# A hybrid decoder layer: the turn of x through six PSUM tiles, dt as one operand, and the SSD diagonal with features on partitions

## The chip, the cores and the metric

The kernel runs on one core of a Trainium2 chip. The core has five engines that run side by side and meet at semaphores: TensorE (PE, with its weight loads as PEld), VectorE (DVE), ScalarE (ACT), GpSimd (POOL) and SyncE (SP), which issues the DMAs here. [...] The metric is the device time of one execution in microseconds, as a median of several runs; the profile is of one further execution.

## The reference, cut to what matters

One layer over 16 learned meta tokens and 1024 tokens, width 1024, all in float32:

```python
xn = rms_norm(h, mix_pre_g)
proj = xn @ w_in                    # z, xBC, dt, q, k, v
# SSD (Mamba-2): 16 heads of 64, 2 groups, state 128, chunks of 128
xbc = silu(causal_dwconv(xbc, conv_w, conv_b))       # xs, B, C
dt = softplus(dt_raw + dt_bias); A = -exp(a_log)
Xdt = xs * dt; Acs = cumsum(dt * A, within a chunk)
Ldec = where(causal, exp(Acs[l] - Acs[s]), 0)
y_diag = einsum('bclgn,bcsgn,bgjcls,bcsgjp->bclgjp', C, B, Ldec, Xdt)
states = einsum(B, exp(Acs[-1] - Acs), Xdt)          # then a scan over the chunks: prev
y_off = einsum(C, prev, exp(Acs))
y_ssd = rms_norm((y_diag + y_off + xs * d_skip) * silu(z), ssd_norm_g)
y_sb = rms_norm(stick_breaking_attention(q, k, v), sb_norm_g)
h = h + rms_norm(concat(y_ssd, y_sb) @ w_out, mix_post_g)
h = h + rms_norm((gelu(dwconv3(xn2 @ W_g)) * (xn2 @ W_u)) @ w_down, ffn_post_g)
```

## The kernel before, in words

Activations and weights of the projections are split into a high part that PE takes in one pass (float32r) and a low rest, so that each product of two operands becomes three matmuls: high x high, low x high, high x low. Plain float32 matmuls stand in the profile as two records each; a transpose on PE is one record.

**Head.** The 1040 positions are nine tiles (16 meta tokens, then eight tiles of 128). For each (lines 204 to 222) ACT squares the tile and sums, DVE and POOL make the scaling factor (`rstd_of`), DVE writes `xn`, PE turns it in two halves of four 128x128 transposes into a PSUM tile of the tag "tp" (`xtp`, line 219), ACT writes the high part `xh` from there (line 221) and DVE the low rest `xl` (line 222). The tag "tp" has two tiles. In this first stage PSUM holds eight banks in four tags of two: "mm" (projections), "sd" (SSD outputs), "z" (masks and decays) and "tp" (turns).

**Projections.** `load_w` brings a block of 128 columns of weights and splits it (ACT high part, POOL low rest). `project_steps` walks three column chunks of 348, 346 and 346 positions (`CH`), 24 matmuls each, and calls `evac`. The first block is dt, only 16 columns wide; then come B and C of group 0, chunk by chunk in turn with dt. Convolutions over the positions run on DVE (`xbc_steps`, lines 313 and 316), silu on ACT.

**dt.** `dtT` (16 x 1040) is turned to tokens with nine transposes (`tpd`, line 390). Then a chain of some twenty small DVE instructions computes dt = softplus, dt x A (`adt`, tile `s2`, line 419) and its split. `decays()` multiplies `adt` with three triangular or full matrices (`pz_ea`, `pz_de`, `pz_cd`, lines 431 and 432) and takes exponentials on ACT. `fill` is a flow of projections of x blocks (`X`), of which two steps run ahead of `decays()`. `bc[0][1][0]()` turns B to tokens (`to_tokens`: `tt_B`, lines 324 and 329, three PSUM tiles of tag "tp", each copied by DVE at line 325 or 330).

**SSD scans.** Two groups of eight heads, nine chunks each (a meta chunk of 16 rows, eight of 128). `scan_steps` runs `chunk_weights(c + 1)`, `chunk_outputs(c)`, `chunk_store(c)` in turn, with steps of projections between. `chunk_weights` makes the decay mask (`sgh` on ACT, `sgl` on POOL, `sg` on PE, exp on ACT into `em`), multiplies it by the masked C.B products (`cb`, `cbm`) on DVE, and makes `xdt` (DVE) and `yo` = xs x d_skip (POOL); `em`, `xdt` and `yo` have two buffers each. `chunk_outputs` makes the state (`xw` on DVE, `st` on PE into a tile of tag "sd", `pv` on POOL and DVE), the diagonal (`yd`, line 507: eight matmuls with `em` as the stationary operand, 128 x 128, and 64 moving columns of `xdt`, into a tile of tag "sd"), adds it to `yo` on DVE (line 508), and the part from the state before (`yf`, line 511, also tag "sd"; `yt` and an addition on DVE). `chunk_store` turns `yo` to features (four transposes, `yt`, line 525), multiplies by silu(z) from `zk`, stores and sums squares.

**Order.** In this part of the kernel a scheduler sets each engine's order from the dependences and its own estimates; each engine then runs its queue strictly in order. From the attention on, PE's order is written by hand.

**Behind it** come eight head pairs of attention (a masked scan on DVE), the output projection, the norms, the up projections, the gated convolution and the down projections.

Of the kernel before, what the change touches and what calls it, by code (L numbers as in the profile page):

```python
# [8 lines left out]
F32 = mybir.dt.float32  # L9
# [7 lines left out]
P = 128  # L17
# [22 lines left out]
WB = 3  # L40
# [11 lines left out]
def tile_layer(ctx: ExitStack, tc: tile.TileContext, x, meta, rows, parts,  # L52
# [148 lines left out]
    with tc.tile_pool(name="pre", bufs=3, side="right") as pre:  # L201
        gpre = row_bcast(pre, 0, D, "gpre")
        for i in range(NT + 1):
            nr = NM if i == 0 else P
            c0 = 0 if i == 0 else NM + (i - 1) * P
            xt = pre.tile([P, D], F32, tag="xt", name=f"xt{i}", bufs=9)
            nc.sync.dma_start(out=xt[:nr], in_=meta if i == 0 else x[(i - 1) * P:i * P, :])
            junk = pre.tile([P, D], F32, tag="junk", name=f"junk{i}", bufs=2)
            ss = pre.tile([P, 1], F32, tag="ss", name=f"ss{i}")
            nc.scalar.activation(junk[:nr], xt[:nr], AF.Square, accum_out=ss[:nr])  # L210
            r = rstd_of(pre, ss[:nr], 1, nr, f"pre{i}")
            xn = pre.tile([P, D], F32, tag="xn", name=f"xn{i}", bufs=2)
            nc.vector.scalar_tensor_tensor(xn[:nr], xt[:nr], r[:nr], gpre[:nr],
                                           op0=ALU.mult, op1=ALU.mult)
            for hf in range(2):
                tp = psum_tp(f"xtp{i}_{hf}")
                for b in range(4):
                    k = 4 * hf + b
                    nc.tensor.transpose(tp[:, b, :nr], xn[:nr, k * P:(k + 1) * P], ident[:nr, :nr])
                dst = (slice(None), slice(4 * hf, 4 * hf + 4), slice(c0, c0 + nr))  # L220
                nc.scalar.activation(xh[dst], tp[:, :, :nr], AF.Copy)
                nc.vector.tensor_tensor(xl[dst], tp[:, :, :nr], xh[dst].bitcast(F32), op=ALU.subtract)
# [81 lines left out]
    with tc.tile_pool(name="ssd", bufs=1, side="right") as sp:  # L304
# [65 lines left out]
        expa = sp.tile([P, 16], F32, name="expa", tag="expa")  # L370
        nc.scalar.activation(expa, alog, AF.Exp)

        dtT = rp.tile([16, L + 3], F32, name="dtT", tag="rt", bufs=1)

        def dt_evac(acc, c0, n):
            nc.vector.tensor_copy(dtT[:, c0:c0 + n], acc[:16, :n])

        head = [project_steps(load_w(w_dt, 16, "dt"), 16, xh, xl, CH, dt_evac, "dt")]
        bc = bc_flow(0)
        head += [steps for steps, _ in bc]  # L380
        for _ in CH:
# [5 lines left out]
        for i in range(NT + 1):  # L387
            nr = NM if i == 0 else P
            c0 = 0 if i == 0 else NM + (i - 1) * P
            nc.tensor.transpose(tpd[:nr, i * 16:(i + 1) * 16], dtT[:, c0:c0 + nr], ident[:16, :16])  # L390
        NA = (NT + 1) * 16

        def t3(name, pool=sp):
# [40 lines left out]
                nc.scalar.activation(dst[:, 1:, :], pz[:, 16:NA].rearrange("p (a b) -> p a b", b=16), AF.Exp)  # L434

        fill = flow([x_flow(0, 0), x_flow(0, 1)], 2)
        run(fill, 2)
        decays()
        tmp.close()
        run(fill, 2)  # L440
        bc[0][1][0]()
        run(fill)

        def chunk_weights(g, c):
# [37 lines left out]
        def chunk_outputs(g, c, em, xdt, yo, prev):  # L482
# [8 lines left out]
            if c < NT:  # L491
# [8 lines left out]
                else:  # L500
# [1 line left out]
                                            prev.rearrange("p (h d) -> p h d", d=64),  # L502
                                            cdec[:, c, hs].unsqueeze(2).to_broadcast([P, 8, 64]), op=ALU.mult)
                    nc.vector.tensor_tensor(nprev, st, nprev, op=ALU.add)
            yg = psum_sd(f"yd{nm}").rearrange("p (h d) -> p h d", d=64)
            for h in range(8):
                mm(yg[:nr, h, :], em[:nr, h, :nr], xdt[:nr, h, :], start=True, stop=True)
            nc.vector.tensor_tensor(yo[:nr], yg[:nr], yo[:nr], op=ALU.add)
            if c > 0:
                yf = psum_sd(f"yf{nm}")  # L510
                mm(yf[:nr], ct[:, c0:c0 + nr], prev, start=True, stop=True)
# [3 lines left out]
                nc.vector.tensor_tensor(yo[:nr], yo[:nr], yt[:nr], op=ALU.add)  # L515
            return yo, zk, nprev

        def chunk_store(g, c, yo, zk):
            nr = NM if c == 0 else P
            c0 = 0 if c == 0 else NM + (c - 1) * P  # L520
            nm = f"{g}_{c}"
            tp = psum_tp(f"yt{nm}")
            yo2 = yo.rearrange("p h d -> p (h d)")
            for b in range(4):
                nc.tensor.transpose(tp[:, b, :nr], yo2[:nr, b * P:(b + 1) * P], ident[:nr, :nr])
            nc.vector.tensor_tensor(zk[:, :, :nr], tp[:, :, :nr], zk[:, :, :nr], op=ALU.mult)
            y0 = M0 if c == 0 else 0
            nc.sync.dma_start(out=yd[c][:, 4 * g:4 * g + 4, :], in_=zk[:, :, y0:nr])
            sqk = sp.tile([P, 4, P], F32, tag="sqk", name=f"sqk{nm}")
            nc.scalar.activation(sqk[:, :, :nr], zk[:, :, :nr], AF.Square)  # L530
            for b in range(0, 4, 2):
                nc.gpsimd.tensor_tensor(sqk[:, b, :nr], sqk[:, b, :nr], sqk[:, b + 1, :nr], op=ALU.add)
            dst = sq[:, c0:c0 + nr]
            if g == 0:
                nc.gpsimd.tensor_tensor(dst, sqk[:, 0, :nr], sqk[:, 2, :nr], op=ALU.add)
            else:
                nc.gpsimd.tensor_tensor(sqk[:, 0, :nr], sqk[:, 0, :nr], sqk[:, 2, :nr], op=ALU.add)
                nc.gpsimd.tensor_tensor(dst, dst, sqk[:, 0, :nr], op=ALU.add)

        def scan_steps(g):  # L540
# [3 lines left out]
            for c in range(NT + 1):  # L544
                nxt = chunk_weights(g, c + 1) if c < NT else None
                yield
                yo, zk, prev = chunk_outputs(g, c, *cur, prev)
                yield
                chunk_store(g, c, yo, zk)
                cur = nxt  # L550

        run(flow([x_flow(0, b) for b in range(2, 4)] + [(z_steps(0, b), []) for b in range(4)], 2))
# [1079 lines left out]
```

## Time and profile before

| | us |
|---|---|
| median of three runs | 1834.47 |
| lowest and highest | 1833.14 and 1835.4 |
| profiled execution, its own time | 1832.72 |
| its span, first to last instruction | 1831.0 |

The rows of the profile are read as follows. A row by stage gives the stretch in us from the span's start, its length, then for PE, PEld, DVE, ACT and POOL the busy time and in brackets the instructions, then the granted clock of TensorE as a share, the mean busy share of the DMA engines and GB/s. A row of waits gives the engine, tile and line that waited, then who ended it: the total, how often, the longest. A row in order of time gives the start, the duration, the engine, the line, the operation, the output <- the inputs, the forms and how many were merged; in brackets stands the idle time ahead of it and what ended it. For a matmul the pair before the form is contraction rows x stationary columns, and the form is rows x moving columns. Matmuls overlap, so two starts are compared rather than durations.

### The profile page before, as it was taken

The page shows a single profiled execution, that of the slowest core. Times are in us where ns is not written, and L with a number is a line of the kernel's source. Part 1 is how long each engine was busy: PE and PEld are TensorE (multiplying, and loading weights), DVE is VectorE, ACT ScalarE, POOL GpSimd, SP SyncE. Part 2 cuts the span into 40 slices and gives each one's busy share as a digit, 9 for nine tenths or more (in the row PEclk, how much of TensorE's full clock was granted, in tenths as well). Part 3 has the DMA queues.
Part 4 walks back from the last instruction along what each step waited for, and adds up shares of the span by engine and source line. Part 5 has one row for each costly group of instructions (what it writes and reads, how often), then busy time and mean ns, then how long its engine had stood idle before and what let it go on. Part 6 is the DMA issues. An engine that isn't in the chain of part 4 may idle for free.

```text
span 1831.0 us, 27362 instructions
## 1 busy us (share of the span) xinstructions
PE 1758.9 (96%) x10957; PEld 1508.3 (82%) x10957; DVE 1060.3 (58%) x1142; ACT 829.0 (45%) x1371; POOL 858.5 (47%) x613
## 2 busy tenths in 40 slices
PE   6899999999999999999799989899999999999997
PEld 5899889889888888888478767788889998888886
DVE  5551783574534544544722256766666666667988
ACT  5333454443655655655654243443333333344444
POOL 3213563485644644643764132276777776600001
PEclk9999999999999999999899999999999999999999
DMA  4123242231011110110232455233233333196344
GB/s 155 47 70 119 75 125 96 71 103 54 24 36 36 32 39 28 32 36 11 82 106 70 139 175 181 81 104 92 87 103 111 104 103 99 52 316 230 95 120 160
DMA packets 91443, 173.96 MB, mean 95 GB/s; under 512 B 11722, under 2 KB 36714, under 8 KB 91316
## 3 DMA queue, kind: packets, MB, share of 16 engines
q1 hardware_dynamic: 91316, 172.21, 29.9%
q8 instruction: 86, 1.41, 0.3%
q14 instruction: 41, 0.34, 0.1%
HBM read 122.39 MB, written 49.79 MB: 94 GB/s over the span
## 4 chain that ended last, share of the span: by engine, by line
PE 47%; DVE 3%; ACT 2%; POOL 1%; issue 1%; DMA 1%; POOLq 0%; SPq 0%; ACTq 0%; DVEq 0%
PE dn L1445 11%; PE fX L1054 9%; PE mo L759 6%; PE fY L1054 6%; PE fA L1054 6%; PE tw L617 1%; PE av L631 1%; PE z L596 1%; PE pj_v L163 1%; PE pj_q L163 1%; PE halo L708 1%; PE pj_k L163 1%; DVE oxn L912 1%; DVE mb L903 1%; POOL yl L749 0%
## 5 line engine op out<-in xcount | busy, mean ns | idle before, releaser
L601 DVE TENSOR_TENSOR_SCAN kp<-kp,hold 128x272 f32<-128x272 f32 (+7 forms) x128 | 206.7, 1657 | 202.3 <-ACT kp L597 99.6
L603 POOL TENSOR_TENSOR bt<-bt,kp 128x256 f32<-128x256 f32 (+7 forms) x128 | 213.8, 1688 | 195.9 <-DVE kp L601 143.3
L997 POOL TENSOR_TENSOR wl<-wr,wh 128x1024 fp32r<-128x1024 f32 x44 | 110.7, 2524 | 40.7 <-ACT wh L996 40.7
L1445 PE MATMUL dn<-dl,dh 128*128 128x512 f32 x308 | 120.1, 390 | 0.1
L1445 PE MATMUL dn<-dh 128*128 128x512 f32 x308 | 120.1, 390 | 0.0
L1445 PE MATMUL dn<-dh,dl 128*128 128x512 f32 x308 | 120.0, 390 | 0.0
L1491 POOL TENSOR_TENSOR fms<-fms,nhalf 128x1 f32<-128x1 f32 x8 | 8.5, 1060 | 225.8 <-DMA ar<-fda 186.0
L597 ACT ACTIVATE kp<-z 128x288 f32<-128x288 f32 (+6 forms) x112 | 82.7, 738 | 60.4 <-PE z L596 37.3
L1374 ACT ACTIVATE dh<-ar 128x512 fp32r<-128x512 f32 x77 | 48.7, 632 | 111.2 <-PE dn L1445 88.9
L996 ACT ACTIVATE wh<-wr 128x1024 fp32r<-128x1024 f32 x44 | 46.6, 1060 | 114.9 <-PE fX L1054 68.3
L596 PE MATMUL z<-k,q 64*128 64x144 f32 (+6 forms) x448 | 88.0, 494 | 8.3 <-ACT bt L598 3.9
L1126 DVE SCALAR_TENSOR_TENSOR ga<-gr,pp,ga 128x1024 f32<-128x1024 f32 x44 | 71.4, 1622 | 34.7 <-ACT ga L1119 34.0
L619 ACT ACTIVATE th<-tw 128x1024 f32<-128x1024 f32 (+2 forms) x96 | 74.4, 811 | 33.2 <-PE tw L617 31.1
L598 ACT ACTIVATE bt<-z 128x288 f32<-128x288 f32 (+6 forms) x112 | 83.0, 741 | 0.0
L617 PE MATMUL tw<-ident,bt 128*128 128x128 f32 x576 | 78.3, 282 | 4.4 <-POOL bt L603 2.9
L631 PE MATMUL av<-th,v 128*64 128x128 f32 x1152 | 78.1, 281 | 0.0
L631 PEld LDWEIGHTS av<-th,v 128*64 128x64 f32 x1152 | 62.6, 138 | 18.1 <-issue 17.3
L1375 DVE TENSOR_TENSOR dl<-ar,dh 128x512 fp32r<-128x512 f32 x77 | 53.2, 691 | 41.9 <-ACT dh L1374 41.8
L617 PEld LDWEIGHTS tw<-ident,bt 128*128 128x128 f32 x576 | 62.9, 143 | 15.9 <-issue 10.6
L596 PEld LDWEIGHTS z<-k,q 64*128 64x128 f32 x448 | 37.8, 191 | 39.0 <-issue 15.8
L1445 PEld LDWEIGHTS dn<-dh 128*128 128x128 f32 x308 | 57.8, 188 | 12.3 <-ACT dh L1374 0.3
L1445 PEld LDWEIGHTS dn<-dl,dh 128*128 128x128 f32 x308 | 57.9, 188 | 12.2 <-DVE dl L1375 0.4
(542 smaller groups left out, 5797.1 us busy)
## 6 DMA issues: line engine op xcount, KB each, us to landing
wr<-in_w_up SPq DMA_DIRECT2D x44, 512.0 KB
fds<-ga SPq DMA_DIRECT2D x44, 256.0 KB
b<-in_w_down SPq DMA_DIRECT2D x44, 256.0 KB
ar<-fds SPq DMA_DIRECT2D x44, 256.0 KB
fda<-ga SPq DMA_DIRECT2D x33, 256.0 KB
ar<-fda SPq DMA_DIRECT2D x33, 256.0 KB
yk<-yd SPq DMA_DIRECT2D x16, 512.0 KB
zd<-zt SPq DMA_DIRECT2D x8, 520.0 KB
```

Of the source, the lines that this page charges most:

```text
L596: mm(z[:, j, :w], q[h, t0:t0 + P], k[h, a:a + w], start=True, stop=True)
L597: nc.scalar.activation(kp[:, :, a:a + w], z[:, :, :w], AF.Sigmoid, scale=-QSCALE)
L598: nc.scalar.activation(bt[:, :, a:a + w], z[:, :, :w], AF.Sigmoid, scale=QSCALE)
L601: nc.vector.tensor_tensor_scan(kp[:, j][:, ::-1], kp[:, j][:, ::-1], hold[:, L - n:L][:, ::-1], 0.0, op0=ALU.mult, op1=ALU.max)
L603: nc.gpsimd.tensor_tensor(bt[:, j, 0:m], bt[:, j, 0:m], kp[:, j, 1:m + 1], op=ALU.mult)
L617: nc.tensor.transpose(tw[:, j, b, :], bt[:, j, c0:c0 + P], ident)
L619: nc.scalar.activation(th[:, :, :nb, :], tw[:, :, :nb, :], AF.Copy)
L631: mm(av[halves[j], :], v[:, kb, halves[j]], th[:, j, b, :], start=kb == 0, stop=kb == i)
L759: mm(acc, u[:, k, :], v[:, cs], start=(k == 0 and j == 0), stop=(k == 7 and j == 2))
L997: nc.gpsimd.tensor_tensor(l, raw, h.bitcast(F32), op=ALU.subtract)
L1054: mm(acc[:, c, :nn], u[:, k, :], v[:, k, c0:c0 + nn], start=first and k == 0 and j == 0, stop=k == 3 and j == 2, skip_group_check=not first)
L1445: mm(banks[t], u[:, 0, c], v[:, 1, :], start=(p == 0 and i == 0), stop=(p == NPR - 1 and i == 2))
```

## The change

Four things change.

1. **x in rotation.** The halves of x are turned into tiles of the tags "tp", "z" and "sd" in rotation, six PSUM tiles in place of two.
2. **dt as one operand.** High and low part of dt's weights stand side by side in one stationary operand of 32 columns, so 16 matmuls do the work of 24 in each chunk of positions. The 16 x 16 matrix pair `fold` (two identities on top of each other) adds both halves in the turn to tokens, which becomes a plain matmul (line 406 after).
3. **Later decays.** Four steps of `fill` and the turn of B now run ahead of `decays()`.
4. **The SSD diagonal with features on partitions.** The product is left out of `chunk_outputs` with its addition on DVE. In `chunk_store` the eight matmuls have `xdt` as the stationary operand (128 x 64) and `em` as the moving one, and write features x tokens straight into the two halves of the partitions of `tp`; the four transposes of `yo` are accumulated on top.

```diff
-                tp = psum_tp(f"xtp{i}_{hf}")
+                tp = (psum_tp, psum_z, psum_sd)[(2 * i + hf) % 3](f"xtp{i}_{hf}")
+                if (2 * i + hf) % 3:
+                    tp = tp.rearrange("p (a b) -> p a b", b=P)
...
-        dtT = rp.tile([16, L + 3], F32, name="dtT", tag="rt", bufs=1)
-
-        def dt_evac(acc, c0, n):
-            nc.vector.tensor_copy(dtT[:, c0:c0 + n], acc[:16, :n])
-
-        head = [project_steps(load_w(w_dt, 16, "dt"), 16, xh, xl, CH, dt_evac, "dt")]
+        dtT = rp.tile([32, L + 3], F32, name="dtT", tag="rt", bufs=1)
+        fold = sp.tile([32, 16], F32, name="fold", tag="fold")
+        nc.vector.tensor_tensor(fold, ident[:32, 0:16], ident[:32, 16:32], op=ALU.add)
+
+        def dt_steps():
+            raw = wp.tile([P, KB, 16], F32, tag="wraw", name="wr_dt")
+            hl = wp.tile([P, KB, 32], F32R, tag="whi", name="wh_dt", bufs=WB)
+            nc.sync.dma_start(out=raw, in_=w_dt)
+            nc.scalar.activation(hl[:, :, 0:16], raw, AF.Copy)
+            nc.gpsimd.tensor_tensor(hl[:, :, 16:32], raw, hl[:, :, 0:16].bitcast(F32), op=ALU.subtract)
+            for c0, n in CH:
+                acc = psum_mm(f"pj_dt_{c0}")
+                for k in range(KB):
+                    for j, src in enumerate((xh, xl)):
+                        mm(acc[:32, :n], hl[:, k, :], src[:, k, c0:c0 + n],
+                           start=(k == 0 and j == 0), stop=(k == KB - 1 and j == 1))
+                nc.vector.tensor_copy(dtT[:, c0:c0 + n], acc[:32, :n])
+                yield
+
+        head = [dt_steps()]
...
-            nc.tensor.transpose(tpd[:nr, i * 16:(i + 1) * 16], dtT[:, c0:c0 + nr], ident[:16, :16])
+            mm(tpd[:nr, i * 16:(i + 1) * 16], dtT[:, c0:c0 + nr], fold, start=True, stop=True)
...
-        run(fill, 2)
+        run(fill, 4)
+        bc[0][1][0]()
         decays()
         tmp.close()
-        run(fill, 2)
-        bc[0][1][0]()
         run(fill)
...
-            yg = psum_sd(f"yd{nm}").rearrange("p (h d) -> p h d", d=64)
-            for h in range(8):
-                mm(yg[:nr, h, :], em[:nr, h, :nr], xdt[:nr, h, :], start=True, stop=True)
-            nc.vector.tensor_tensor(yo[:nr], yg[:nr], yo[:nr], op=ALU.add)
...
-        def chunk_store(g, c, yo, zk):
+        def chunk_store(g, c, em, xdt, yo, zk):
...
             for b in range(4):
-                nc.tensor.transpose(tp[:, b, :nr], yo2[:nr, b * P:(b + 1) * P], ident[:nr, :nr])
+                for j in range(2):
+                    mm(tp[halves[j], b, :nr], xdt[:nr, 2 * b + j, :], em[:nr, 2 * b + j, :nr],
+                       start=b == 0, stop=False, skip_group_check=True)
+            for b in range(4):
+                mm(tp[:, b, :nr], yo2[:nr, b * P:(b + 1) * P], ident[:nr, :nr], start=False, stop=True,
+                   is_transpose=True, skip_group_check=True)
...
-                chunk_store(g, c, yo, zk)
+                chunk_store(g, c, cur[0], cur[1], yo, zk)
```

How the scheduler orders the changed program can be read from the built program without running it; the prediction uses that order. PE now turns tiles 0 to 6 ahead of dt's first matmul; ahead of `pz_ea` it runs all 24 matmuls of the second X block's first chunk and the first five transposes of B, and the last four transposes of B follow one matmul after `pz_de`. On DVE the copy of B's first turn stands behind three steps of the first X convolution. On ACT the exponential of `pz_ea`, the silu of the first X block and the exponentials of `pz_de` and `pz_cd` follow one another. In the scans the eight matmuls of the diagonal and the four transposes stand where the four transposes stood; on DVE `xdt` of two chunks on stands behind the last addition to `yo`.

## The prediction

> **What bounds the kernel now.** I read the busy shares first, then busy time by stage, then who TensorE (PE) waits for, then the instructions in order of time around each wait.
>
> ```profile
> PE 1758.9 (96%) x10957; PEld 1508.3 (82%) x10957; DVE 1060.3 (58%) x1142; ACT 829.0 (45%) x1371; POOL 858.5 (47%) x613
> ```
> ```profile
> 0.00:20.00 20.00, 4.94 (x24) 4.06 (x24) 9.45 (x23) 12.34 (x22) 5.74 (x18) 1.00 0.80 273
> 20.00:40.00 20.00, 17.41 (x97) 14.19 (x98) 14.41 (x20) 10.53 (x19) 8.48 (x6) 1.00 0.26 79
> 40.00:60.00 20.00, 20.00 (x129) 17.07 (x128) 1.85 (x4) 3.24 (x7) 0.00 (x0) 1.00 0.01 2
> ...
> 80.00:100.00 20.00, 15.11 (x83) 13.86 (x82) 11.82 (x20) 7.72 (x21) 3.35 (x3) 0.83 0.10 27
> ...
> 200.00:250.00 50.00, 47.23 (x295) 42.39 (x294) 41.53 (x48) 29.81 (x60) 31.73 (x26) 1.00 0.34 98
> ```
> ```profile
> PE xtp L219 <- DVE xl L222: 6.0, 4, 2.2
> PE pz_ea L431 <- DVE s L419: 4.9, 1, 4.9
> ...
> PE pj_X L163 <- ACT craw_X L310: 0.5, 1, 0.5
> ```
> ```profile
> PE yf L511 <- DVE pv L504: 2.9, 2, 2.0
> PE cb L469 <- ACT ct L318: 2.0, 1, 2.0
> PE st L496 <- DVE xw L493: 0.8, 1, 0.8
> PE yd L507 <- DVE em L472: 0.5, 1, 0.5
> ```
> PE is busy 96% of the span, so in the region that the diff touches (0 to 440 us) two things count: PE work taken away, and PE idle time. The stages give 15.1 us of idle in the first 20 us, 2.6 in the next and 4.9 in 80:100; the waits name their causes: 6.0 us for the second half of the split of x (L222), 4.9 for the dt chain (L419), and 6.2 in the scans (the last four rows). Behind 440 us PE's instruction order is the same in both kernels, so I let what is won early pass to the end undiminished.
>
> **The x turn (rotation) and dt, as far as B's third chunk.**
>
> ```profile
> 12.48 1.97 PE L219 MATMUL xtp<-ident,xn 128*128 128x128 f32 x8 [1.12 <-DVE xl L222]
> 16.63 1.94 PE L219 MATMUL xtp<-ident,xn 128*128 128x128 f32 x8 [2.19 <-DVE xl L222]
> ...
> 23.47 0.47 PE L163 MATMUL pj_dt<-xh,wh_dt 128*16 128x348 f32 x1 [0.88 <-ACT wh_dt L150]
> ...
> 27.16 0.49 PE L163 MATMUL pj_dt<-xh,wh_dt 128*16 128x348 f32 x1
> 27.45 0.49 PE L163 MATMUL pj_dt<-xl,wh_dt 128*16 128x348 f32 x1
> ...
> 30.34 0.41 PE L163 MATMUL pj_dt<-xh,wh_dt 128*16 128x348 f32 x1
> ...
> 33.71 0.63 PE L219 MATMUL xtp<-ident,xn 128*128 128x128 f32 x4 [0.59 <-DVE xl L222]
> ```
> ```profile
> 62.34 0.32 PE L163 MATMUL pj_B<-xl,wh_B 128*128 128x346 f32 x1
> 62.50 0.32 PE L163 MATMUL pj_B<-xh,wl_B 128*128 128x346 f32 x1
> ```
> ```profile
> 13.35 1.28 DVE L213 SCALAR_TENSOR_TENSOR xn<-xt,rs_pre,gpre 128x1024 f32<-128x1024 f32 x1 [0.51 <-POOL rs_pre L190]
> 15.81 1.28 DVE L222 TENSOR_TENSOR xl<-xtp,xh 128x512 fp32r<-128x512 f32 x2
> ```
> Warm, projection matmuls start 0.159 us apart (62.34, 62.50); until 30.34 they start 0.29 apart (27.16, 27.45), a half clock that the granted clock of the stage (1.00) does not show. Between 33.71 and 62.66 PE never waits: 166 matmuls (26.4 us) and 24 transposes, so 0.106 each.
>
> The changed order has PE turn tiles 0 to 6 first, then 16 dt matmuls where 24 stood; up to the same point remain 168 matmuls and 16 transposes, 26.7 + 1.7 = 28.4 us. When does that begin? With six PSUM tiles a turn no longer waits for the split before it, only for xn. DVE's new order from 13.35 on is five xn (1.25 each with overlap), three split pairs (1.28) and five small scalings (about 0.14): 10.8 us; for three more waits like the 0.51 on POOL I add 1.5, and tile 6 is normalised at 25.7. Its turn at the slow 1.94 ends at 27.6, so B's third chunk ends at 56.0 if the clock is up. Before, it was down from the first matmul at 23.47 to 30.34, 6.9 us. I take half of that again after 27.6: 3.4 us at half rate cost 1.6, so 57.6 against 62.66, a gain of **5.1**. The small addition that builds fold costs nothing: it stands on DVE behind the last split of x, where DVE is busy 1.85 us of 20 (40:60). Of the 5.1, 24 x 0.159 = 3.8 are dt's missing matmuls. Ends: no cold stretch and a start 1.5 earlier give 8.1; all 6.9 cold and a start 1.5 later 2.0.
>
> [...]
>
> **The later decays.**
>
> ```profile
> 66.57 0.68 PE L390 MATMUL tpd<-ident,dtT 16*16 16x16 f32 x9
> ...
> 85.63 0.23 PE L431 MATMUL pz_ea<-s,tri 16*16 16x16 f32 x2 [4.89 <-DVE s L419]
> ```
> ```profile
> 85.27 0.31 DVE L419 SCALAR_TENSOR_TENSOR s<-dt,expa 128x144 f32<-128x144 f32 x1
> ...
> 86.96 2.66 DVE L316 SCALAR_TENSOR_TENSOR xsT<-craw_X,pp,xsT 128x1040 f32<-128x1040 f32 x2
> ...
> 101.72 0.28 DVE L325 COPY xtk<-tt_X 16x128 f32<-16x128 f32 x1 [6.07 <-PE tt_X L324]
> ```
> ```profile
> L296 PE MATMUL pta<-ones,sq x18: 163/250/271, 454.9 to 456.7; 128*128 128x1 f32 x16, 128*2 128x1 f32 x2
> ```
> ```profile
> 74.40 1.28 ACT L408 ACT_TABLE_LOAD   x1
> ```
> The dt chain runs on DVE from B's last chunk on and ends at 85.58, 22.9 behind it; nothing in the change shortens it, so it ends 5.1 earlier and no more. In before's times PE came to pz_ea at 80.74; it now does 17 more matmuls (2.7) and five transposes of B (0.5) ahead of pz_ea, the nine turns of dt become plain fp32 matmuls (18 records like pta, 1.9 us where 0.68 stood) and the 0.47 wait is swallowed. PE arrives near 84.7 and waits 0.9, not 4.9. But a new wait follows: the last four transposes of B need the PSUM tile of B's first turn, whose copy now stands on DVE behind two convolution steps (86.96 + 2.66), so until 89.9. PE has one matmul in between. From there 47 matmuls, four transposes, pz_cd (0.5, estimated from pz_ea) and the first turn of X take 8.6: X's first copy at 98.5 against 101.72, 3.2 better. The old stall left the clock at 0.83 for that stage (3.4 us lost); with 0.9 and about 2.7 idle close together a cold stretch may come back. I take half, **1.6**. Ends: 3.2, and -1.3 if also the two more activation tables that ACT now loads (exp, silu, exp; 1.28 each) come into the path.
>
> **The SSD diagonal.**
>
> ```profile
> 364.54 1.08 PE L511 MATMUL yf<-pv,ct 128*128 128x512 f32 x2
> ...
> 371.70 1.89 PE L507 MATMUL yd<-xdt,em 128*128 128x64 f32 x16
> 373.44 1.08 PE L511 MATMUL yf<-pv,ct 128*128 128x512 f32 x2
> ```
> ```profile
> 558.25 1.31 PE L631 MATMUL av<-th,v 128*64 128x128 f32 x20
> 559.50 1.53 PE L617 MATMUL tw<-ident,bt 128*128 128x128 f32 x12
> 560.78 0.41 PE L163 MATMUL pj_q<-xh,wh_q 128*128 128x346 f32 x1
> ```
> A chunk's 16 records (eight heads, two passes) take 373.44 - 371.70 = 1.74 us with 128 stationary columns and 64 moving. The new form, 64 stationary and 128 moving with the halves of the output in turn, is exactly that of av: 20 records in 1.25 us, 0.0625 each, so 1.00. That is 0.74 less in each of 16 full chunks, **11.8** us; the two 16-row chunks I leave at nothing. The four turns stay four. What speaks against it is a change of shape between av-like matmuls and transposes, twice more a chunk; in the attention twelve transposes behind av take 1.28, 0.107 each, with the change in it.
>
> [...]
>
> DVE's addition of yd (18 x 0.68 us) goes too, which PE feels only through its waits. The wait of st for xw (0.8) goes, as xw moves ahead of two convolution steps; that of yd for em (0.5) goes, as the product now comes later. The yf waits (2.9) came from yf taking st's PSUM tile, not yet read by pv; with yd gone, st and yf keep a tile each. But DVE is no sooner: pv, yt, xw and yo still follow it, and PE meets them at the turn of yo. Counting both chunks through, 1.3 and 0.3 come back there. So 4.2 becomes 1.6, **2.6** won; ends 0 and 4.2. The wait for ct (2.0) stays.
>
> **Sum.** 5.1 + 1.6 + 11.8 + 2.6 = 21.1. From the profiled execution's 1832.72 us (span 1831.0) that is 1811.6; the median lies 1.75 above that execution, so I say 1813.
>
> **Rivals.**
> *The head gives nothing*: cold clock after the turns and again after the decays. For it: the half clock until 30.34 and the 0.83. Against it: PE has less idle in both places. 2.0 - 1.3 in place of 6.7: 1819.
> *The shape changes cost*: each switch exposes a transpose's latency instead of its pitch.
>
> ```profile
> L617 PE MATMUL tw<-ident,bt 128*128 128x128 f32 x576 | 78.3, 282 | 4.4 <-POOL bt L603 2.9
> ```
> 282 - 107 = 0.17 us, twice in 16 chunks is 5.5: 1819. [...]
> *The new matmuls are no faster* (the change doesn't do what it says): if not the stationary width but the record itself sets 0.109, 11.8 falls away: 1825; with the first rival too, 1831.
> *Slower: DVE paces the scans.* xdt and em now keep their two buffers until PE's turn, and xdt of two chunks on waits there in DVE's queue ahead of zk, cbm, pv, em, yt, xw and yo, on which the next turn waits.
>
> ```profile
> 215.18 2.92 DVE L472 TENSOR_TENSOR em<-em,cbm 128x1024 f32<-128x1024 f32 x1
> ...
> 372.58 1.79 DVE L472 TENSOR_TENSOR em<-em,cbm 128x1024 f32<-128x1024 f32 x1
> ```
> In the second scan I count 7.0 us round that loop against PE's 8.90 a chunk (364.54 to 373.44) less 0.74. It decides once the loop passes 8.16, and makes the whole slower beyond about 9.3. With em as long as at 215.18 and xdt wholly in the loop it is 9.9: 16 x 1.0 - 6.7 = +9.3, 1844. Against it: em took 1.79 in that scan.
> *Better*: warm throughout and no wait left, 8.1 + 3.2 + 11.8 + 4.2: 1807.
>
> **How the numbers follow.** Forecast 66% (1809 to 1817), head nothing 12%, shape changes 8%, matmuls no faster 4%, that with the first 2%, slower 4%, better 4%. From 1806 to 1823 all but some 12% is held. No change can be told below 0.2%, 3.7 us: faster 0.94, same 0.02, slower 0.04.
>
> **What would show it.** Right: PE's waits for xl gone and B's last chunk ending near 57 to 58; a short wait at pz_ea and one of 2 to 3 us at the last turn of B; a yt group of 16 records in 1.0 us; no wait of yf for pv, small ones at yt. Wrong: records 0.1 us apart in that group, matmuls 0.29 apart behind the turns beyond 31, PE waiting at yt in every chunk, or stages behind 440 us that grow.

## The result and the profile after

| | before | after |
|---|---|---|
| median | 1834.93 | 1813.7 |
| lowest and highest | 1833.14 and 1836.56 | 1811.23 and 1817.08 |
| profiled execution (its span) | 1832.72 (1831.0) | 1814.51 (1812.8) |

The ratio is 0.9886, with an interval of 0.9867 to 0.9905: 21 us off 1835, and the forecast of 1813 holds. It does not hold term by term. Below stand the rows of the profile after that answer to those shown of before, in the same order of columns: the busy shares, two stages, and who PE waits for (first 0 to 110 us, then 110 to 445).

```profile
PE 1746.0 (96%) x10942; PEld 1492.9 (82%) x10942; DVE 1060.6 (59%) x1125; ACT 831.4 (46%) x1373; POOL 859.7 (47%) x613
```
```profile
20.00:40.00 20.00, 16.40 (x104) 15.13 (x105) 14.84 (x23) 10.88 (x21) 9.11 (x8) 0.91 0.27 81
80.00:100.00 20.00, 17.66 (x106) 16.56 (x106) 11.56 (x14) 10.40 (x24) 3.40 (x3) 0.91 0.18 39
```
```profile
PE xtp L221 <- DVE xn L213: 6.4, 4, 4.0
PE tt_B L331 <- DVE bn L327: 2.3, 1, 2.3
```
```profile
PE yt L540 <- DVE yo L526: 2.5, 3, 1.2
PE cb L484 <- ACT ct L320: 2.0, 1, 2.0
PE sg L480 <- POOL sgl L473: 0.2, 1, 0.2
```

PE lost 12.9 us of busy time (1758.9 to 1746.0), which leaves 5.3 of the 18.2 us between the two spans to waits. The wait for `xl` is gone and one of nearly its size for `xn` has taken its place; the 4.9 at `pz_ea` is gone; the 2.3 at `tt_B` is the new wait that was forecast; `yt` waits for `yo`.

The instructions in order of time, in the head and in one chunk of the first scan:

```profile
22.54 4.42 PE L221 MATMUL xtp<-ident,xn 128*128 128x128 f32 x24 [4.00 <-DVE xn L213]
26.72 0.40 PE L389 MATMUL pj_dt<-xh,wh_dt 128*32 128x348 f32 x1
26.96 0.32 PE L389 MATMUL pj_dt<-xl,wh_dt 128*32 128x348 f32 x1
27.11 0.32 PE L389 MATMUL pj_dt<-xh,wh_dt 128*32 128x348 f32 x1
...
56.40 0.32 PE L163 MATMUL pj_B<-xh,wl_B 128*128 128x346 f32 x1
...
83.70 1.12 PE L331 MATMUL tt_B<-ident,bt 128*128 128x128 f32 x4 [2.34 <-DVE bn L327]
...
85.19 0.49 PE L163 MATMUL pj_X<-xh,wh_X 128*128 128x346 f32 x1
85.48 0.49 PE L163 MATMUL pj_X<-xl,wh_X 128*128 128x346 f32 x1
...
198.71 1.09 PE L537 MATMUL yt<-em,xdt 128*64 128x128 f32 x16
199.74 0.66 PE L540 MATMUL yt<-ident,yo 128*128 128x128 f32 x4
200.15 0.48 PE L480 MATMUL sg<-sgh,lowr 128*128 128x512 f32 x1
```
```profile
94.20 0.28 DVE L327 COPY xtk<-tt_X 16x128 f32<-16x128 f32 x1 [8.14 <-PE tt_X L326]
```

dt's matmuls start 0.16 apart almost at once. B's last matmul starts 6.1 earlier (56.40 against 62.50), X's first copy 7.5 (94.20 against 101.72). Behind the wait at `tt_B` matmuls stand 0.29 apart (85.19, 85.48), where the granted clock is 0.50 (85 to 87): half rate. The diagonal's 16 records take 199.74 - 198.71 = 1.03 us where they took 1.74.

The same landmarks in every kernel tell where time goes. Each column is the difference of two starts in the order of time: of B's last matmul from the span's start; from there to X's first copy; on to the first `st`; the first scan, to the first turn of the second B; on to the first `cb` of the second scan; the second scan, to the turn of the first `edge` behind it; and the rest of the span.

| | B | X | first st | scan 1 | cb | scan 2 | rest |
|---|---|---|---|---|---|---|---|
| before | 62.5 | 39.2 | 87.5 | 153.4 | 12.5 | 85.3 | 1390.6 |
| after | 56.4 | 37.8 | 86.3 | 145.1 | 12.5 | 82.2 | 1392.5 |
| c_again | 57.2 | 38.7 | 86.3 | 145.1 | 12.5 | 79.5 | 1393.2 |
| p1_rot | 60.2 | 38.6 | 87.5 | 153.4 | 12.6 | 86.9 | 1391.3 |
| p2_dt | 59.0 | 39.1 | 87.5 | 153.4 | 12.5 | 85.3 | 1390.5 |
| p3_decay | 64.4 | 38.2 | 86.3 | 155.5 | 12.5 | 86.9 | 1391.8 |
| p4_diag | 62.5 | 38.5 | 87.5 | 145.1 | 12.5 | 79.5 | 1391.7 |
| u_nodecay | 56.8 | 38.1 | 87.5 | 145.1 | 12.5 | 82.2 | 1395.0 |
| v_ct | 56.4 | 37.8 | 86.3 | 145.1 | 11.2 | 78.7 | 1391.7 |
| v_both | 56.2 | 34.4 | 86.3 | 145.1 | 11.2 | 78.7 | 1390.5 |
| w_wide | 57.1 | 38.9 | 86.3 | 149.7 | 12.5 | 88.6 | 1392.7 |
| h_runs | 56.3 | 37.8 | 86.3 | 148.1 | 12.5 | 81.9 | 1393.6 |
| d_xdt3 | 56.6 | 37.8 | 86.3 | 145.1 | 12.6 | 79.5 | 1395.6 |
| f_both_xdt3 | 57.1 | 34.5 | 86.3 | 145.1 | 11.2 | 79.8 | 1393.7 |

### The profile page after: what moved, and what is told of

It reads as the page before. It is cut to its first block, busy times and chain, and to the rows that moved or that the text cites. A ratio compares the mean times of both kernels' runs of the same rounds, so it can differ in the third digit from the quotient of the medians.

```text
span 1812.8 us, 27316 instructions
## 1 busy us (share of the span) xinstructions
PE 1746.0 (96%) x10942; PEld 1492.9 (82%) x10942; DVE 1060.6 (59%) x1125; ACT 831.4 (46%) x1373; POOL 859.7 (47%) x613
## 4 chain that ended last, share of the span: by engine, by line
PE 47%; DVE 3%; ACT 2%; DMA 2%; POOL 1%; issue 1%; POOLq 0%; SPq 0%; ACTq 0%; DVEq 0%
PE dn L1461 11%; PE fX L1070 9%; PE mo L775 6%; PE fY L1070 6%; PE fA L1070 6%; PE tw L633 1%; PE av L647 1%; PE z L612 1%; PE pj_v L163 1%; PE pj_q L163 1%; PE pj_k L163 1%; DVE oxn L928 1%; DMA yk<-yd 1%; DVE mb L919 1%; POOL yl L765 0%
## 5 line engine op out<-in xcount | busy, mean ns | idle before, releaser
L1391 DVE TENSOR_TENSOR dl<-ar,dh 128x512 fp32r<-128x512 f32 x77 | 53.3, 692 | 41.8 <-ACT dh L1390 41.8
L612 PEld LDWEIGHTS z<-k,q 64*128 64x128 f32 x448 | 37.3, 189 | 38.6 <-issue 15.9
L765 POOL TENSOR_TENSOR yl<-yk,yh 128x1024 fp32r<-128x1024 f32 x16 | 38.8, 2428 | 61.9 <-ACT yh L764 61.9
L1461 PEld LDWEIGHTS dn<-dl,dh 128*128 128x128 f32 x308 | 57.8, 188 | 12.5 <-DVE dl L1391 0.4
```

The lines of the kernel that those rows point to most:

```text
L612: mm(z[:, j, :w], q[h, t0:t0 + P], k[h, a:a + w], start=True, stop=True)
L1461: mm(banks[t], u[:, 0, c], v[:, 1, :], start=(p == 0 and i == 0), stop=(p == NPR - 1 and i == 2))
```

## The experiments

### One part at a time on the kernel before

The edits are the four parts of the diff, each alone.

> The kernel before with only the rotation of the x turns through six PSUM tiles. Theory (the parts add up): of the 6.1 us by which the last chunk of B ends earlier in the changed kernel (56.56 against 62.66), 3.8 are the 24 missing dt matmuls, so the rotation alone makes it end 2.3 earlier, near 60.4, and the whole 2.3 us shorter (ratio 0.9987). PE's waits for xl go, waits for xn of about 6 us in all take their place, and the first dt matmuls are 0.16 us apart. Rival (the rotation helps only with the shorter dt): the end of the last chunk of B stays within 0.7 of 62.66 and the time stays the same (ratio 1.000).

> The kernel before with only dt as one operand of 32 columns and the fold. Theory: 24 matmuls of 0.159 us go, so the last chunk of B ends 3.8 earlier, near 58.9. Some of the missing matmuls ran at half rate before (until 30.34), so it may be up to 5. The 18 records of the fold (2.1 us where 0.68 stood) lie ahead of the wait for the dt chain and cost nothing. Whole: 3.8 shorter (ratio 0.9979). Rival (PE waits longer for the x turns instead, the dt matmuls having filled that time): the last chunk of B ends 1 to 2 earlier only, ratio 0.9992.

> The kernel before with only the decays moved behind the second chunk of X and the first turns of B. Theory: the 4.9 us wait for the dt chain shrinks to 0 to 0.5, a wait of about 2.3 at the last turn of B appears with a half-rate stretch of some 2.4 us behind it. X's first copy comes 1.4 to 2.8 earlier than 101.72, near 99.6, and the whole is as much shorter (ratio 0.9989). Rival (the later order gives nothing, the gain seen in the changed kernel comes from the earlier start of the dt chain): X's first copy within 0.5 of 101.72, ratio 1.000.

> The kernel before with only the SSD diagonal with features on partitions. Theory: the first 100 us as before; the 16 records of a chunk 1.03 us where 1.74 stood, 16 full chunks, 11.4 us; 0.9 of that given back by the turns (0.41 against 0.35), and some 2 us of waits (xw, em, yf) won: scans end 12 to 14 earlier, whole 12.5 shorter (ratio 0.9932). Rival 1 (the early parts and this one need each other, because DVE is short): less than 9 us, ratio 0.995 or more. Rival 2 (part of the gain is lost again behind the scans): the scans end 12 to 14 earlier but the whole is under 10 shorter.

| | median | ratio to before | interval |
|---|---|---|---|
| before | 1835.55 | | |
| p1_rot | 1833.18 | 0.9989 | 0.9980 to 0.9999 |
| p2_dt | 1832.25 | 0.9988 | 0.9974 to 1.0001 |
| p3_decay | 1836.9 | 1.0008 | 0.9997 to 1.0018 |
| p4_diag | 1822.28 | 0.9930 | 0.9915 to 0.9946 |

B's last matmul in p1_rot, and dt's first and B's last in p2_dt, in order of time:

```profile
60.16 0.32 PE L163 MATMUL pj_B<-xh,wl_B 128*128 128x346 f32 x1
```
```profile
24.43 0.50 PE L387 MATMUL pj_dt<-xh,wh_dt 128*32 128x348 f32 x1 [1.69 <-POOL wh_dt L382]
...
58.97 0.32 PE L163 MATMUL pj_B<-xh,wl_B 128*128 128x346 f32 x1
```

The rotation moves it by 2.3, dt by 3.5, and both together by 6.1: they add up, as the theory had it, within the 0.8 by which two executions of the changed kernel differ (56.4 and 57.2). In p1_rot the waits for `xl` are gone and 7.3 us of waits for `xn` have taken their place, where about 6 were expected. By the medians alone p1_rot is just clear of noise and p2_dt is not: its interval takes in 1. dt falls short of 3.8, and a wait shows where: dt's first matmul (24.43) now needs POOL's low half of the weights too and waits 1.69 where it waited 0.88 for ACT alone.

The diagonal alone gives 12.8 us (0.0070 x 1835.55), as expected of the theory, and needs none of the other parts. Its scans end 14.8 us earlier, more than the 12 to 14 expected, as a half-rate stretch of before is absent from its second scan (see below); 1.1 of the 14.8 come back behind the scans. The rival that part of it is lost again behind the scans would have left under 10.

The later decays alone are no faster: by the time the rival holds. By the trace neither does: X's first copy comes at 102.57, not near 99.6 and not within 0.5 of 101.72, and PE still waits 1.7 at `pz_ea` where 0 to 0.5 were expected. Counted from B's last matmul, the trace does show a gain: 1.0 us as far as X's first copy and 1.2 from there to the first `st`. The second was not in the prediction at all. In the kernel before PE waits for the silu of the first X block:

```profile
110.77 0.28 PE L324 MATMUL tt_X<-ident,xsT 128*16 128x128 f32 x1 [1.06 <-ACT xsT L318]
```

With the decays later this wait is gone, in p3_decay and in every kernel with that part. What the profiled execution of p3_decay loses again lies elsewhere: 1.9 us ahead of B's last matmul, 2.1 in the first scan, 1.6 in the second and 1.2 behind it. In the first scan the clock is down:

```profile
188.00:192.00 4.00, 4.00 (x30) 2.92 (x30) 1.96 (x2) 1.41 (x2) 1.99 (x1) 0.97 0.00 0
192.00:196.00 4.00, 4.00 (x18) 4.00 (x17) 4.00 (x5) 0.00 (x0) 1.84 (x2) 0.61 0.42 131
```

One execution can't say whether that comes with the later decays or by chance; the next runs bear on it.

### The changed kernel again, without the later decays, and without two of its waits

The decays were put back for u_nodecay. The other two edits:

```diff
         fill = flow(qkv_flow(p) for p in range(8))
+        run(fill, 1)
         for i, _ in enumerate(scan_steps(1)):
-            run(fill, int(i % 4 != 1 and i % 8 != 3))
+            run(fill, int(i % 4 != 1 and i % 8 != 3 and i < 18))
```
```diff
-                tp = psum_tp(f"tt_{nm}_{part}")
+                if nm == "B0" and part == 2:
+                    tp = psum_sd(f"tt_{nm}_{part}").rearrange("p (a b) -> p a b", b=P)
+                else:
+                    tp = psum_tp(f"tt_{nm}_{part}")
```

v_ct has the first, v_both both.

> The changed kernel as it is, as the measure for the three runs beside it: ratio to before near 0.9886. Its trace shows what differs from one execution to the next with the same code: theory (the clock's half-rate stretches come in pieces of about 3.4 us, and whether a short wait brings none, one or two of them depends on when it falls): the half-rate stretch behind the wait for ct in the second scan (6.7 us in the first profile of this kernel, a granted clock of 0.72 over 12 us) is now 0, 3.4 or 6.8. Rival (a given wait costs a given stretch): again 6.7.

> The changed kernel with the decays back where they were (ahead of the second chunk of X). Theory: the later decays are worth 2.2 to 2.6 us (as alone: 1.0 from the last chunk of B to the first copy of X, 1.2 from there to the first scan, which the one execution of that run lost again to a half-rate stretch in the scan): the wait at pz_ea is 4.4 to 5 us again, the first st comes at 183 instead of 180.5, whole 2.4 slower than the changed kernel (ratio to it 1.0013). Rival (the later decays give nothing or cost, as the time of that run alone, 1.5 us above before, would have it): the same as the changed kernel, or up to 2 faster.

> The changed kernel with one step of the attention's projections (24 matmuls, 3.8 us) put ahead of the second scan and taken out of its end, so that PE has work while ct is made. Theory (the second scan fell short by the wait for ct and by the clock that follows it): the wait of 2.0 for ct goes and with it the half-rate stretch behind it, which cost 0 to 3.4 in the executions seen (3.4 in the first profile of the changed kernel). From the first turn of the second B to the end of the scans 94.7 becomes 89 to 91; whole 2 to 5.4 faster than the changed kernel, 3.7 as the middle (ratio to it 0.998). Rival (DVE or ACT sets that stretch): the wait only moves to em, xw or yo, and the whole is within 1 us of the changed kernel.

> The run before (a projection step ahead of the second scan), and also the last four turns of the first B into a PSUM tile of the sd pair instead of tp, so that they need not wait for the copy that stands behind two convolution steps. Theory: the wait of 2.3 at tt_B goes too, and the half-rate stretch of 2.4 behind it: 2.3 to 3.5 more, so 4.3 to 8.9 faster than the changed kernel, 6.5 as the middle (ratio to it 0.9964, to before near 0.985). Rival (X's chain on DVE and ACT sets the pace there): the first copy of X stays at 94 and the wait reappears at the turns of X; no more than the run before.

| | median | lowest and highest | ratio to before | interval |
|---|---|---|---|---|
| before | 1836.48 | 1833.98 and 1838.22 | | |
| c_again | 1813.38 | 1810.49 and 1814.1 | 0.9871 | 0.9854 to 0.9889 |
| u_nodecay | 1816.81 | 1815.65 and 1818.95 | 0.9896 | 0.9881 to 0.9912 |
| v_ct | 1810.0 | 1808.28 and 1812.38 | 0.9859 | 0.9843 to 0.9875 |
| v_both | 1806.8 | 1803.99 and 1810.29 | 0.9842 | 0.9823 to 0.9860 |

**The clock behind a wait.** The 12 us behind the wait for `ct`, by the stage's row (the last number but two is the granted clock), in before, in after and in the same kernel once more:

```profile
355.12:367.12 12.00, 11.46 (x70) 9.31 (x71) 8.81 (x15) 7.58 (x21) 7.19 (x8) 0.86 0.13 34
```
```profile
338.10:350.10 12.00, 12.00 (x63) 9.43 (x64) 8.83 (x13) 7.76 (x21) 6.68 (x8) 0.72 0.18 45
```
```profile
339.72:351.72 12.00, 11.50 (x88) 9.61 (x89) 11.39 (x14) 9.10 (x23) 8.27 (x9) 1.00 0.20 45
```

At half rate, 0.86 is 0.14 x 12 x 2 = 3.4 us, 0.72 is 6.7, and 1.00 is none. The same wait of 2.0 us was followed by one piece, two and none, so the rival that a given wait costs a given stretch falls. The second scan takes 82.2 us with two and 79.5 with none, with the same instructions in the same order. The two time-lines agree: in after the `st` of the first full chunk takes 1.91 (344.16), in c_again 1.02 (343.89).

```profile
344.16 1.91 PE L511 MATMUL st<-xw,bn 128*128 128x512 f32 x2
```
```profile
343.89 1.02 PE L511 MATMUL st<-xw,bn 128*128 128x512 f32 x2
```

In the traces of before and after all sixteen stretches in which the granted clock is 0.50 last 3.4 or 6.8 us. In after two pieces followed a wait of 2.0 us with records of 16 rows beside it.

A half-rate piece came without any wait, too. In after PE never waits between 32.3 and 81 us. The turn of dt with `fold`, now 18 plain records of 16 columns, takes 2.0 us, and 0.7 us behind it the clock is down for 3.4:

```profile
60.47 2.09 PE L406 MATMUL tpd<-fold,dtT 32*16 32x16 f32 x18
```
```profile
63.20:66.60 3.40, 3.40 (x14) 3.40 (x13) 3.40 (x3) 0.00 (x0) 1.16 (x1) 0.50 0.32 118
```

The same piece stands in six of the ten executions with `fold` (not in c_again, w_wide, f_both_xdt3 and p2_dt) and in none of the four without. So the new turn of dt costs more than its 1.4 us of records in some executions, by up to 1.7. No run was made to separate these records from the chance of the clock.

**The waits themselves.** With PE's work put ahead of it, the wait for `ct` shrinks to 0.76 in v_ct and the clock stays at 1.00 behind it; from the turn of the second B to the end of the scans 94.7 (after) or 92.0 (c_again) become 89.9. The median is 3.4 lower than c_again's, as expected (3.7), though the ranges overlap. With the second edit X's first copy comes 3.6 earlier relative to after:

```profile
90.59 0.28 DVE L330 COPY xtk<-tt_X 16x128 f32<-16x128 f32 x1 [4.73 <-PE tt_X L329]
```

and v_both is 6.6 us below c_again, with no run in common; 6.5 was expected. The new wait at `tt_B` was thus worth some 3 us, its 2.3 and the half rate behind it. Some half of the 6.6 is clock: the granted clock of v_both's runs is 0.9885 in the mean and that of the changed kernel's eight runs 0.9868, which is an estimated 3 us of 1810. **v_both is faster than both kernels.**

**The later decays.** u_nodecay is 3.4 us slower than c_again, where 2.4 was expected, with no run in common; it does share a range with the four runs of after, the same kernel (1811.23 to 1817.08). Its wait at `pz_ea` came back with 2.7 only, the stage ahead of it having run in part at half rate. Its trace does not carry the 3.4: the first `st` comes at 182.41, against 180.47 in after and 182.12 in c_again. The granted clocks of the runs tell more. In the mean it is 0.9853 in u_nodecay and 0.9868 in the changed kernel's eight runs, and 0.9861 in p3_decay against 0.9876 in the 29 runs of before beside it. That is an estimated 2.7 us of lost clock in each pair. Without it the later decays are worth about 1 us in the changed kernel and 1.4 on top of the kernel before, near the traces' 1.2 for the wait at `tt_X`. Since once the kernel with the later decays has the lower clock and once the one without, the lower clock does not follow from them. So the rival that they give nothing is unlikely, and a size of 3.4 is not shown.

### The diagonal: width or alternation

```diff
-                    mm(tp[halves[j], b, :nr], xdt[:nr, 2 * b + j, :], em[:nr, 2 * b + j, :nr],
-                       start=b == 0, stop=False, skip_group_check=True)
+                    mm(tp[:, b, :nr], xdt.rearrange("p h d -> p (h d)")[:nr, b * P:(b + 1) * P],
+                       em[:nr, 2 * b + j, :nr],
+                       start=b == 0 and j == 0, stop=False, skip_group_check=True)
```
```diff
-            for b in range(4):
-                for j in range(2):
+            for j in range(2):
+                for b in range(4):
                     mm(tp[halves[j], b, :nr], ...
```

The first is w_wide, the second h_runs.

> The changed kernel, but each matmul of the diagonal takes the two heads of a pair as its stationary operand, 128 columns instead of 64, and writes all 128 partitions; this mixes the heads of a pair, so the SSD part of the output is not the reference's. Moving operand, count of records and turns stay. Theory (the width of the stationary operand sets the record): the 16 records take 1.74 us again (0.109 each) instead of 1.03, in 16 full chunks 11.4 us, whole near 1825, ratio to before 0.9937. The turns behind them take 0.35 again instead of 0.41 if the change of shape costs anything, and 0.41 if it does not. Rival (it was the moving side or where the output goes): 1.0 to 1.1 us, and the time of the changed kernel.

> The changed kernel with the loops over the pair and over its two heads exchanged: the eight records that write the upper half of the partitions come first, then the eight of the lower half, where they took turns two by two. Theory A (the narrower stationary operand alone makes the record short): the 16 records still take 1.0 to 1.1 us, time that of the changed kernel. Theory B (it is the alternation of the halves, one half loading or working while the other works): 16 records towards 1.7 us, in 16 full chunks up to 11 us more, 1820 to 1825.

| | median | ratio to before | interval |
|---|---|---|---|
| w_wide | 1825.89 | 0.9943 | 0.9928 to 0.9959 |
| h_runs | 1817.98 | 0.9903 | 0.9887 to 0.9919 |

One chunk of the first scan in w_wide, then in h_runs:

```profile
201.60 1.95 PE L537 MATMUL yt<-em,xdt 128*128 128x128 f32 x16
203.38 0.60 PE L541 MATMUL yt<-ident,yo 128*128 128x128 f32 x4
203.74 0.48 PE L480 MATMUL sg<-sgh,lowr 128*128 128x512 f32 x1
```
```profile
198.90 1.58 PE L537 MATMUL yt<-em,xdt 128*64 128x128 f32 x16
200.41 0.66 PE L540 MATMUL yt<-ident,yo 128*128 128x128 f32 x4
200.83 0.48 PE L480 MATMUL sg<-sgh,lowr 128*128 128x512 f32 x1
```

With 128 columns the 16 records take 203.38 - 201.60 = 1.78 us, 0.111 each; with 64 columns but one half of the partitions after the other 1.51; with 64 columns and the halves in turn 1.03. These are means over a group. The first 0.45 us of a group, in after, h_runs and w_wide, show how many records have started by then (the count at the end of a row):

```profile
198.71 0.66 PE L537 MATMUL yt<-em,xdt 128*64 128x128 f32 x8
```
```profile
198.90 0.65 PE L537 MATMUL yt<-em,xdt 128*64 128x128 f32 x4
```
```profile
201.60 0.72 PE L537 MATMUL yt<-em,xdt 128*128 128x128 f32 x5
```

While h_runs writes one half alone, its narrow records are no denser than the wide ones of w_wide. The starts of the single records say it more exactly. In w_wide they are 0.11 apart throughout. In after they come in pairs, at 0, 6, 160, 166, 269, 276, 378 and 385 ns and so on: two trains of eight, each with a step of 0.109 us behind a first step of 0.160, side by side. In h_runs one train of eight runs from 0 to 816 ns with the same steps, and the second starts at 495, when five of the first have started. So a record costs 0.109 with 64 columns and 0.111 with 128, and narrowness alone gives 0.002. All of the 0.75 us a chunk comes from two trains at once: in after all along, in h_runs only where the second overlaps the first, which is the 0.27 that h_runs still wins. Theory B of h_runs holds, and its 1.7 was too much only because the trains overlap. The forecast for w_wide came true (1825.89, near 1825), but not by its theory: w_wide changes the width and the place of the output at once and could not tell them apart. That each train is one half of the partitions is inferred from the order of the loops; the profile does not list the half. The scans of h_runs are 3.0 and 2.4 longer than c_again's, not 16 x 0.48 = 7.7, as PE's waits for `yo` fall from 2.7 to 0.2 us. The whole is 4 to 5 us slower.

The change of shape has a cost, in three places. The first step of a train is 0.160 instead of 0.109, the first turn starts 0.20 behind the last record where w_wide has 0.11, and the four turns take 0.41 instead of 0.36. That is 0.2 us a chunk, of which 0.14 lies inside the 1.03.

### Three buffers for `xdt`

```diff
-            xdt = sp.tile([P, 8, 64], F32, tag="xdt", name=f"xdt{nm}", bufs=2)
+            xdt = sp.tile([P, 8, 64], F32, tag="xdt", name=f"xdt{nm}", bufs=3)
...
-        e, s, s2 = (t3(n, tdp) for n in ("e1", "s1", "s2"))
+        es = sp.tile([P, 4, P], F32, tag="sqk", name="es").rearrange("p a b -> p (a b)")
+        e, s, s2 = (es[:, n * NA:(n + 1) * NA].rearrange("p (a b) -> p a b", b=16) for n in range(3))
```

> The changed kernel with three buffers for xdt instead of two; the room comes from three temporaries of the dt chain, which are put into the tile of sqk. Theory (what is left of the waits at the turn of yo comes from DVE's queue, where xdt stands until PE has done with the chunk before): DVE's waits of xdt for the diagonal's matmuls (16.5 us in both scans) fall to near 0, PE's waits of yt for yo from 1.2 to 2.7 to under 1, whole 0.5 to 2 faster than the changed kernel. Rival (DVE's own work sets yo: two convolution steps of 2.7 and a mask multiplication of up to 2.9 ahead of it): the waits of xdt go, those of yt stay at 1.2 to 2.7, whole within 0.7.

> All three together: the projection step ahead of the second scan, the last turns of the first B in the sd pair, three buffers for xdt. Theory: the 6.6 us below the changed kernel that the first two gave, and 0.5 to 2 more: near 1806, ratio to before 0.9836. Rival (the third does nothing): 1806.8, ratio 0.9842.

d_xdt3 took 1813.33 (0.9877, 0.9858 to 0.9895), f_both_xdt3 1807.19 (0.9841, 0.9821 to 0.9860): nothing gained on c_again and v_both. DVE's waits of `xdt` for the diagonal fell from 16.5 (after) or 15.2 (c_again) to 13.6 only, so the third buffer did not do what it was put in for, and PE's for `yo` stayed:

```profile
PE yt L541 <- DVE yo L527: 2.8, 4, 1.2
```

The longest of them (1.2 in both kernels) has its cause in DVE's own work. Its instructions up to `yo` in d_xdt3, in order of time:

```profile
220.49 3.55 DVE L318 SCALAR_TENSOR_TENSOR xsT<-craw_X,pp,xsT 128x1040 f32<-128x1040 f32 x2
223.96 1.48 DVE L488 TENSOR_TENSOR em<-em,cbm 128x1024 f32<-128x1024 f32 x1
225.36 1.50 DVE L318 SCALAR_TENSOR_TENSOR xsT<-craw_X,pp,xsT 128x1040 f32<-128x1040 f32 x1
226.78 0.68 DVE L520 TENSOR_TENSOR pv<-st,pv 128x512 f32<-128x512 f32 x1
...
229.12 0.68 DVE L527 TENSOR_TENSOR yo<-yo,yt 128x512 f32<-128x512 f32 x1
```

No idle time stands in brackets from 220.49 on: three convolution steps and the mask come ahead, and no buffer of `xdt` is in that chain. The rival of this run holds for this wait. The two of 0.64 in the second scan, where `xdt` waited 1.30 and took 2.86 in the first execution, are not settled by it.

## Why the prediction was right, point by point

| step | predicted | after | c_again |
|---|---|---|---|
| as far as B's third chunk | 5.1 | 6.1 | 5.3 |
| from there to X's first copy | 1.6 | 1.4 | 0.6 |
| from there to the first `st` | 0 | 1.2 | 1.2 |
| both scans | 11.8 + 2.6 = 14.4 | 11.4 | 14.1 |
| behind them | 0 | -1.9 | -2.6 |
| sum, against the span of before | 21.1 | 18.2 | 18.6 |

The spans give 18 to 19 us and the medians 21, since the profiled execution of before lies 2.2 under the median of its runs; the forecast of 1813 had allowed 1.75 for that. Execution for execution the forecast was 1811.6, and 1814.5 came. That the median came out within a microsecond of 1813 owes something to luck.

**The head**: the mechanism held (no wait for `xl`, waits for `xn`, dt starting at 26.7 against 27.6), and 3.5 of it are dt's matmuls, 2.3 the rotation. The half of a cold stretch that was taken off after the turns did not come in the first execution. The clock came up during the turns: PE ran turns alone until 26.72, the granted clock is 0.50 in 23 to 25 us, 0.66 in 25 to 26 and 1.00 in 26 to 27, and dt's second and third matmuls are 0.15 apart. In c_again, 5.3, the clock came up 2.5 us later, during dt's first matmul (28.2 against 25.7). So the half cold stretch that the prediction took off is within what two executions show.

**The later decays**: PE came to `pz_ea` at 80.02, behind the end of the dt chain (77.03 + 2.39 = 79.42), so the forecast wait of 0.9 shrank to nothing; it was 1.0 in c_again. The difference is the half-rate piece behind the turn of dt, which after has and c_again has not, and for which the prediction had no term. The wait at B's last turn was 2.34 against 2.7. Behind it after has one half-rate piece and c_again two (granted clock 0.91 and 0.83 in 80:100), which is why 1.4 were won there in one and 0.6 in the other. ACT's two more tables (seven loads of 1.28 us in 20 to 110 us, where before has five) cost PE nothing that the waits show. What was missed is the 1.06 of `tt_X` for the silu: the prediction's list of waits ended at 110 us and began again in the scans.

**The diagonal**: 0.71 won a chunk against 0.74. The size came out because `av`, from which it was read, has the same loops (line 631 before) and the same pairs, its first records starting at 0, 7, 160 and 167 ns. The cause did not. The prediction credited the stationary width and named the halves in turn only as part of the form; the rival's premise, that the record itself takes 0.109, is true within each half, and the rival fails because two halves run at once. The rival of costly shape changes was there too, at 0.2 a chunk instead of 0.34. The rows of `av` show this cost, too: their 1.25 us hold the same first step of 0.160 and the same 0.20 ahead of the first turn, so that most of it was already in the forecast and the 0.05 of the turns was not.

**The waits of the scans** are the term that was mis-sized. `xw`, `em` and `yf` went, as predicted, but 2.5 to 2.7 came back at the turn of `yo`, not 1.6: 4.2 became 2.5 to 2.7 without the 2.0 for `ct`, which stays. And the prediction gave the wait for `ct` no clock. The kernel before has one half-rate piece behind it, after two and c_again none, so that 11.4 is too low and 14.1 too high for the change itself. By the second scan of p1_rot a further piece costs the kernel before 1.6 (86.9 against 85.3). Without its one the kernel before would take an estimated 83.7 there, 4.2 more than c_again; with the 8.3 of the first scan, where no piece stands in any of the three, the scans win 12.5, not 14.4.

**Behind the scans** PE's order is the same, and the stretch took 1390.5 to 1395.6 over fourteen executions. What after and c_again lose there lies in one part of it, between the first `ptb` and the first `x2tp` (the output projection and the norms). It takes 38.7 in before and in v_ct, 41.9 in after and 41.8 in c_again, and the granted clock is the difference (before, after, v_ct):

```profile
1043.17:1081.91 38.74, 36.24 (x161) 24.29 (x158) 16.52 (x20) 14.94 (x23) 9.60 (x5) 1.00 0.60 196
```
```profile
1021.00:1062.89 41.89, 38.62 (x161) 26.05 (x158) 15.95 (x20) 14.95 (x23) 9.61 (x5) 0.92 0.54 180
```
```profile
1018.82:1057.55 38.73, 36.01 (x160) 24.27 (x158) 16.61 (x20) 14.94 (x23) 9.60 (x5) 1.00 0.58 195
```

0.92 is two half-rate pieces (0.08 x 41.9 x 2 = 6.7), around two waits of 1.6 and 1.7 us at `mo`; before has the same two waits, of 0.9 and 1.6, and no piece. The pieces do not come with the new diagonal by necessity, since v_ct and v_both have it and no piece there. But eight of the ten executions with it have one to three pieces in this part, and of the four without it only p3_decay has one. Whether the change makes them likelier is open.

**The slower rival**, DVE setting the pace, did not come: DVE stays at 59% and PE waits for `yo` three times in 16 full chunks.

## What to carry to other kernels

When several matmuls with 64 stationary columns go into one PSUM tile, let neighbours write different halves of the partitions, so that two run at once: here the order of two loops was worth 0.48 us in 1.51, and narrow records one half at a time were no faster than wide ones. Before a mean over a group of records is explained, look at the starts of the single ones. When a step is moved, look first for the wait that takes its place, then for a free PSUM tile or a piece of independent PE work for it: two such edits of a few lines gave a further 6.6 us. And price a wait of some 2 us on PE with what may follow at half rate, 0 to 3.4 us here and 5.1 once, do the same for 2 us of very small records, and compare single traces by stretches, since the same kernel differs by that much from one execution to the next.

## What the runs showed of the hardware that was not expected

The half-rate stretches of before and after come in pieces of 3.4 us, sixteen of one or two pieces (3.4 or 6.8 us). The wait of 2.0 us for `ct` was followed by one in before, by two in after and by none in c_again, with the same instructions around it in these two. 2.0 us of 18 records with 16 columns were followed by one without any wait, in six of ten executions. In w_wide the granted clock behind that wait is 0.57 over 12 us, three pieces (0.43 x 12 x 2 = 10.3):

```profile
344.44:356.44 12.00, 12.00 (x44) 9.15 (x45) 5.64 (x11) 7.70 (x21) 5.25 (x7) 0.57 0.11 24
```

The clock came up while PE ran nothing but turns: in after it is 0.50 in 23 to 25 us and 1.00 in 26 to 27, and dt's first matmul starts at 26.72. And plain float32 records with 128 moving columns start 0.109 us apart with 64 stationary columns and 0.111 with 128, but with 64 two trains of them, one into each half of the partitions, run side by side: 16 in 1.03 us where 16 wide ones take 1.78.
